# A decoder block with two token mixers: the loads of the keys for the gated states move from SP's queue to GpSimd's, and ahead of the first branch's weights

## The chip, the cores and the metric

The kernel runs on one core of a Trainium2 chip. Its time is the device time of one execution in microseconds (us). Before the change it is 1404.6 us, the median of 3 runs (1404.36 to 1404.93).

In what follows PE is TensorE, DVE is VectorE, ACT is ScalarE, POOL is GpSimd and SP is SyncE, which here does nothing but issue DMAs. An engine works off its instructions in the order in which they stand, and the DMAs that it issues stand in that order too: an instruction whose semaphore isn't there yet holds up all that stand behind it.

## The reference

One layer of a decoder block on 1024 rows of width 1024, in fp32. One input projection feeds two mixers, whose outputs are projected, gated and added.

```python
def mixing_sublayer(xn, w_in, b_gate, w_alpha_up, b_alpha, gla_norm_g, w_branch_sb, w_branch_gla, w_out):
    proj = xn @ w_in
    (sb_q, sb_k, sb_v, g_q, g_k, g_v, g_r, g_a, gate_sb, gate_gla) = jnp.split(proj, offsets, axis=-1)
    o_sb = stick_breaking_attention(...)     # 8 heads of 64, causal, weights are products of sigmoids
    o_gla = gla_chunked(...)                 # 4 heads, states of 64 x 128
    o_gla = o_gla * lax.rsqrt(jnp.mean(o_gla * o_gla, axis=-1, keepdims=True) + EPS)
    o_gla = from_heads(o_gla) * gla_norm_g * jax.nn.silu(g_r)
    y = (jax.nn.sigmoid(gate_sb + b_gate[0]) * (o_sb @ w_branch_sb)
         + jax.nn.sigmoid(gate_gla + b_gate[1]) * (o_gla @ w_branch_gla))
    return y @ w_out

def gla_chunked(q, k, v, log_a):             # per chunk of rows
    q_dec, k_inv, k_to_end = qf * jnp.exp(cum), kf * jnp.exp(-cum), kf * jnp.exp(cum_last - cum)
    o_intra = tril(q_dec @ k_inv.T) @ vf
    d_state = k_to_end.T @ vf                # added to the decayed state, chunk after chunk
    o_inter = q_dec @ states_before
```

The block then is h = x + mixing(rms_norm(x)), h = h + conv_ffn(rms_norm(h)) with 2 x 2816 channels, and a last RMSNorm.

## The kernel before

**Matmuls.** A fp32 product is made of three fp32r matmuls: each operand is split in a high part (a cast on ACT, L119) and the rest (a subtraction on DVE, L110). `mac` (L191, its matmul is L197) does the three products for every 128 rows of the contraction; a half output of 128 x 512 over 512 rows is 12 matmuls, and `branch` issues them as two groups of six.

**Stages.** (1) RMSNorm and the input projection; its outputs go to DRAM, among them `kt_d`, the keys of the gated branch that have been decayed to the end of their chunk (k_to_end). (2) The stick-breaking attention, in `attend`: `weigh`, `turn_weights` and `gather`. `gather` multiplies the weights with the values (L712), adds a bias on ACT (L718) and stores to `osb_d` with SP (L720). After the last head of a half of the rows, `fetch_heads` loads that half back with eight loads (L702), adds two partial sums each (DVE, L116) and splits them into `ob[0]` or `ob[1]`, the right operand of the first branch; `ob[1]` is made from the last two gathers' stores. In between, single steps of `gates` fill PE: the matmuls of the merge gates (L197), a sigmoid (ACT, L588) and a store to `gate_d` (L589). (3) The gated branch: `gated` interleaves `states` (per chunk of 128 rows a matmul on the keys, L808, a copy or an update of the state on DVE, L815 or L817, and a scaled copy on POOL, L819) with `out_pair` (L823 to L883). One `fill(first_branch, ...)` in two of three of its steps adds the first branch's matmuls, `o_sb @ w_branch_sb`. (4) `branch(1, ...)`, the output projection and the FFN.

**What sets the order around the change.** The code runs once to record the instructions; the order in which Python calls things is the order on each engine, except that the gates' matmuls are recorded at a lower priority (`tc.high_priority(offset=-LATER)`), so a scheduler may move them back behind others. Generators (`gate_steps`, `first_branch`) are drawn on with `fill(steps, n)`, which takes n steps. Between the end of `attend` and `gated` stand these lines:

```python
    first_branch = branch(0, ob, w_branch_sb)
    fill(first_branch, 1)
    fill(gate_steps, BEFORE)
    fetch_rest()
    fill(gate_steps, 128)
```

The first step of `first_branch` asks for the first branch weights (512 KB, `load`, L173, on SP) and makes two pieces of them (`piece`, L119 on ACT, L110 on DVE). `fetch_rest` asks for the keys: two loads of 512 KB from `kt_d` (L800), with `nc.sync.dma_start`, so in SP's queue. `gates` with 128 steps uses up what is left of the gates. `fetch_gated` (L783), called earlier from `gates`, has by then asked for the values, the decayed queries and the inverse keys on POOL's queue (L788, L790, L791).

**Buffers.** Keys, branch weights, gate weights and the attention's weights all take a buffer of the same tag, `t4` (128 x 1024 fp32); who asks first gets the one that came free first, and its load waits until the last reader of that buffer is done.

Of the kernel before, what the change touches and what calls it, by code (L numbers as in the profile page):

```python
# [17 lines left out]
P = 128  # L18
# [28 lines left out]
SPOT = 0  # L47
SOON = 1
FFN_FROM = 18
BEFORE = 4  # L50
PAIR_SKEW = 3
GLA = 2, 3
WAIT = 1, 1, 5, 4, 1
# [12 lines left out]
def block_kernel(ctx: ExitStack, tc: tile.TileContext, x, norm_mix_g, w_in, b_gate, w_alpha_up, b_alpha,  # L66
                 gla_norm_g, w_branch_sb, w_branch_gla, w_out, norm_ffn_g, w_ffn_in, conv_w, conv_b,
                 w_ffn_out, norm_final_g, out):
    nc = tc.nc
# [17 lines left out]
    def t8(dt=F32R):  # L87
        return sb.tile([P, 2 * D], dt, tag="t8", name=nm("t8"), bufs=16)

    def t4(dt=F32):  # L90
        return sb.tile([P, D], dt, tag="t4", name=nm("t4"), bufs=T4)

    def t2(dt=F32):
        return sb.tile([P, HALF], dt, tag="t2", name=nm("t2"), bufs=T2)

    def bank():
        return ps.tile([P, HALF], F32, tag="bank", name=nm("bank"), bufs=8)

    def dram(name, rows, cols, dt=F32):
        return dp.tile([rows, cols], dt, tag=name, name=name)  # L100

    def by(a, k):
        return a.rearrange("p (k c) -> p k c", k=k)

    def quarter():

        return [by(t8(), 4) for _ in range(2)]
# [4 lines left out]
    def mul(o, a, b):  # L112
        nc.vector.tensor_tensor(out=o, in0=a, in1=b, op=ALU.mult)

    def add(o, a, b):
        nc.vector.tensor_tensor(out=o, in0=a, in1=b, op=ALU.add)  # L116

    def split(h, l, src):
        nc.scalar.copy(h, src)  # L119
        sub(l, src, h.bitcast(F32))  # L120
# [38 lines left out]
    qd_d, ki_d, kt_d = (dram(n, GH * GK, S) for n in ("qd_d", "ki_d", "kt_d"))  # L159
# [6 lines left out]
    def fill(steps, n):  # L166
        for _ in range(n):
            next(steps, None)


    def load(src, k, room=None):
        raw = by((t4() if room is None else room)[:, 0:k * src.shape[1]], k)
        nc.sync.dma_start(raw, src.rearrange("(k p) c -> p k c", p=P))  # L173
        return raw
# [5 lines left out]
    def piece(src):  # L180

        v = t4(F32R)
        h, l = v[:, 0:HALF], v[:, HALF:]
        k = src.shape[1] if len(src.shape) == 3 else 1
        split(*((h, l) if k == 1 else (by(h, k), by(l, k))), src)
        return by(h, 4), by(l, 4)
# [4 lines left out]
    def mac(w, r, k=4, pt=None, start=True, stop=True):  # L191

        pt = bank() if pt is None else pt
        (wh, wl), (rh, rl) = w, r
        for kk in range(k):
            for m, (a, b) in enumerate(((wh, rh), (wh, rl), (wl, rh))):
                nc.tensor.matmul(pt, a[:, kk], b[:, kk], start=start and kk == 0 and m == 0,  # L197
                                 stop=stop and kk == k - 1 and m == 2)
        return pt
# [355 lines left out]
    def gates():  # L555

        def raw(n):
            if n < len(order):
                g = order[n][0]
                return load(w_in[:, C_GATE + g * P:C_GATE + (g + 1) * P], NK)  # L560

        gs = range(N_GATES, 2 * NK)
        order = [(g, (0,)) for g in gs[:N_HALVES]]
        order += [(g, (0, 1)) for g in gs[N_HALVES:]] + [(g, (1,)) for g in gs[:N_HALVES]]
        nxt = raw(0)
        ws = piece(nxt[:, :4]), piece(nxt[:, 4:])
        coming = None
        yield
        for n, (g, halves) in enumerate(order):
            if n == len(order) - N_HALVES:  # L570
                r = None
                for a in ("11", "12"):
                    del xq[a]
                fetch_gated()
            nxt = raw(n + 1)
            for half in halves:
                pt = bank()
                for kh in range(2):
                    for k in (0, 2):
                        w, r = ([a[:, k:k + 2] for a in v] for v in (ws[kh], xq[f"{half + 1}{kh + 1}"]))  # L580
                        with tc.high_priority(offset=-LATER):
                            mac(w, r, 2, pt, start=kh == 0 and k == 0, stop=kh == 1 and k == 2)
                        if half == halves[-1] and nxt is not None and 2 * kh + k // 2 == SOON:
                            coming = piece(nxt[:, :4]), piece(nxt[:, 4:])
                        if (kh, k) != (1, 2):
                            yield
                sg = t2()
                nc.scalar.activation(sg, pt, AF.Sigmoid, bias=col(V_BG, g))  # L588
                nc.scalar.dma_start(gate_d[g * P:(g + 1) * P, half * HALF:(half + 1) * HALF], sg)  # L589
                yield  # L590
            ws = coming

    gate_steps = gates()
# [200 lines left out]
    def fetch_rest():  # L794

        small = [by(t2(), 4) for _ in range(2)]
        state.extend((v[:, 0], v[:, 1]) for v in small)
        for p in range(2):
            kt = t4()
            nc.sync.dma_start(kt, kt_d[p * P:(p + 1) * P, :])  # L800
            gla[p] += by(kt, NT), by(t4(), NT)

    def states(p, n0, n1):
# [106 lines left out]
    def branch(b, o, w):  # L910

        def pieces(i):
            if i < NK:
                if i % 2 == 0:
                    raws.append(load(w[:, i * P:(i + 2) * P], 4))
                return piece(raws[-1][:, :, i % 2 * P:(i % 2 + 1) * P])

        raws = []
        nxt = [pieces(i) for i in range(2)]
        yield  # L920
        for n in range(2 * NK):
            i, th = n // 4 * 2 + n % 2, n // 2 % 2
            if n % 4 == 0:
                wps, nxt = nxt, []
            elif n % 4 > 1:
                nxt.append(pieces(i + 2))
            wp = wps[i % 2]
            sg = t2()
            g = b * NK + i
            nc.sync.dma_start(sg, gate_d[g * P:(g + 1) * P, th * HALF:(th + 1) * HALF])  # L930
            if i % 4 == 0:
                if b == 0:
                    yb[th, i // 4] = by(t8(F32), 4)
                else:
                    yq[th, i // 4] = quarter()
            pt = bank()
            mac([a[:, 0:2] for a in wp], [a[:, 0:2] for a in o[th]], 2, pt, stop=False)
            yield
            mac([a[:, 2:4] for a in wp], [a[:, 2:4] for a in o[th]], 2, pt, start=False)
            y = yb[th, i // 4][:, i % 4]  # L940
            if b == 0:
                mul(y, pt, sg)
            else:
                mul(sg, pt, sg)
                add(sg, sg, y)
                split(*(a[:, i % 4] for a in yq[th, i // 4]), sg)
            yield
# [34 lines left out]
    for w in attend():  # L982
        owed += w + EACH
        done += w
        rate = FILL[done > 3 * NT * (NT + 1) // 2 * SBH // 4]
        while owed >= rate:
            owed -= rate
            fill(gate_steps, 1)
    first_branch = branch(0, ob, w_branch_sb)
    fill(first_branch, 1)  # L990
    fill(gate_steps, BEFORE)
    fetch_rest()
    fill(gate_steps, 128)
    xq.clear()
    og = [quarter() for _ in range(2)]
# [320 lines left out]
```

## Time and profile before

| | |
|---|---|
| median of 3 runs | 1404.6 us (1404.36 to 1404.93) |
| profiled execution, its own time | 1404.87 us |
| its span in the profile | 1403.2 us |
| mean granted clock of TensorE | 0.996 |
| busy: PE, DVE, ACT, POOL | 1372.2, 1063.9, 643.6, 128.8 us |
| loads of the keys (L800) | 2 of 512 KB on SP's queue, 7.0 us from issue to landing |
| the first of them issued, landed | 547.88, 554.85 us from the span's start |

The profile is that of one execution. Each view gives places in us from the start of the span. A row of the timeline has start, length, engine, line, operation, output and input, the count, and in brackets how long the engine had been idle and what it waited for. A row of waits has the engine and the tile that waited, the operation waited for, then the sum, the count and the longest. In the chain that ended last each row is a piece of time and what it was spent in; "SPq L702" is SP issuing a DMA of line 702. A row of windows has the stretch, its length, the busy time of PE, PEld (weight loads), DVE, ACT and POOL, the granted clock of TensorE as a share of the full one, the busy share of the DMA engines, and GB/s. Matmuls are pipelined: a row's end overlaps with the next one's start.

### The profile page before, as it was taken

To read this page: it belongs to the slowest core of one execution; us is meant where nothing else is said; L and a number is where in the kernel's file an instruction comes from. 1 tells how busy PE (TensorE), PEld (TensorE's weight loads), DVE (VectorE), ACT (ScalarE), POOL (GpSimd) and SP (SyncE) were. 2 spreads that over 40 slices of the span, in tenths; PEclk is the share of its full clock that TensorE was granted. 3 is DMA by queue.
4 is the path that set the end of the run, shared out by engine and by line. 5 is a ranking of instruction groups with operands and counts; after the bars stand their busy time and mean duration, and the time that the engine had idled before them with its cause. 6 is when DMAs were issued, how large, how long until landed. Compare 5 with 4: busy or idle time off the path is not lost.

```text
span 1403.2 us, 18305 instructions
## 1 busy us (share of the span) xinstructions
PE 1372.2 (98%) x6549; PEld 1138.5 (81%) x6549; DVE 1063.9 (76%) x1640; ACT 643.6 (46%) x1242; POOL 128.8 (9%) x223
## 2 busy tenths in 40 slices
PE   7999999999999996999999999999999999999998
PEld 5788888888888875888888788888888888888886
DVE  6388788874878775648447997998888987897855
ACT  6234455653766563543234543333333333454654
POOL 0002133103011000300000000100000000000000
PEclk9999999999999998999999999999999999999999
DMA  6335277448766475464424434563554437953232
GB/s 241 139 97 167 70 231 247 143 157 231 194 150 152 127 223 196 148 213 158 155 91 135 114 96 150 190 217 134 180 181 150 152 108 267 324 176 99 97 106 105
DMA packets 165082, 228.44 MB, mean 163 GB/s; under 512 B 11017, under 2 KB 106379, under 8 KB 164480
## 3 DMA queue, kind: packets, MB, share of 16 engines
q1 hardware_dynamic: 136496, 141.63, 33.0%
q0 software_dynamic: 21920, 71.63, 15.6%
q10 hardware_dynamic: 6576, 14.03, 2.7%
q8 instruction: 51, 0.84, 0.3%
q14 instruction: 39, 0.32, 0.1%
HBM read 160.80 MB, written 66.45 MB: 162 GB/s over the span
## 4 chain that ended last, share of the span: by engine, by line
PE 56%; DVE 3%; DMA 1%; ACT 1%; issue 1%; SPq 0%; POOL 0%; ACTq 0%; DVEq 0%
PE bank L197 34%; PE bank L1179 15%; PE bank L1046 5%; DVE t L110 2%; DVE t L116 1%; DMA t<-kt_d 0%; PE bank L808 0%; DMA t<-gate_d 0%; PE bank L845 0%; DMA t<-in_w_branch_sb_dram 0%; DMA t<-in_w_branch_gla_dram 0%; PE bank L321 0%; PE bank L880 0%; SPq L702 0%; DVE t L313 0%
## 5 line engine op out<-in xcount | busy, mean ns | idle before, releaser
L197 PE MATMUL bank<-t,t 128*128 128x512 f32 x3624 | 862.9, 393 | 0.9 <-DVE t L110 0.8
L197 PEld LDWEIGHTS bank<-t,t 128*128 128x128 f32 x3624 | 677.1, 188 | 143.3 <-DVE t L110 1.6
L110 DVE TENSOR_TENSOR t<-t,t 128x512 fp32r<-128x512 f32 (+3 forms) x663 | 440.3, 697 | 93.9 <-ACT t L119 88.7
L119 ACT CAST t<-t 128x512 fp32r<-128x512 f32 x551 | 325.1, 626 | 342.1 <-DVE t L110 84.0
L116 DVE TENSOR_TENSOR t<-bank,t 128x512 f32<-128x512 f32 x266 | 179.3, 685 | 101.6 <-PE bank L197 58.3
L1179 PE MATMUL bank<-t,t 128*128 128x512 f32 x924 | 209.6, 389 | 0.0
L1179 PEld LDWEIGHTS bank<-t,t 128*128 128x128 f32 x924 | 173.4, 188 | 36.0
L110 DVE TENSOR_TENSOR t<-bank,t 128x512 fp32r<-128x512 f32 (+4 forms) x128 | 72.1, 578 | 33.2 <-ACT t L119 32.8
L367 PE MATMUL bank<-t,t 128*128 128x512 f32 x384 | 91.7, 398 | 1.6 <-ACT t L119 1.5
L1046 PE MATMUL bank<-t,t 128*128 128x512 f32 x384 | 88.9, 391 | 0.0
L116 DVE TENSOR_TENSOR t<-t,t 128x512 f32<-128x512 f32 x115 | 75.5, 685 | 15.8 <-ACT t L497 8.6
L367 PEld LDWEIGHTS bank<-t,t 128*128 128x128 f32 x384 | 72.9, 191 | 17.9 <-ACT t L119 2.2
L1077 ACT ACTIVATE t<-t,vcol 128x1024 f32<-128x1024 f32 x22 | 27.4, 1245 | 128.0 <-DVE t L116 128.0
L110 DVE TENSOR_TENSOR t<-t 128x512 f32<-128x512 f32 x120 | 82.1, 691 | 3.7 <-DMA t<-in_w_ffn_in_dram 3.3
L119 ACT CAST t<-bank 128x512 fp32r<-128x512 f32 (+3 forms) x124 | 61.8, 511 | 49.1 <-PE bank L691 27.3
L1046 PEld LDWEIGHTS bank<-t,t 128*128 128x128 f32 x384 | 71.6, 188 | 14.7
L1079 DVE SCALAR_TENSOR_TENSOR t<-t,vcol,t 128x1023 f32<-128x1023 f32 (+1 forms) x44 | 56.2, 1278 | 14.1 <-ACT t L1077 13.9
L682 DVE TENSOR_TENSOR_SCAN t<-t,t 128x128 f32<-128x128 f32 (+1 forms) x64 | 51.4, 814 | 14.4 <-ACT t L679 13.7
L691 PE MATMUL bank<-ident,t 128*128 128x128 f32 x288 | 53.5, 273 | 1.9 <-ACT t L588 1.3
L677 PE MATMUL bank<-t,t 128*128 128x128 f32 (+3 forms) x192 | 54.6, 368 | 0.1
L712 PE MATMUL bank<-t,t 128*128 128x256 f32 (+1 forms) x320 | 51.1, 276 | 0.4 <-DVE t L110 0.4
L712 PEld LDWEIGHTS bank<-t,t 128*128 128x128 f32 x320 | 46.4, 190 | 2.8 <-DVE t L110 0.6
(142 smaller groups left out, 760.4 us busy)
## 6 DMA issues: line engine op xcount, KB each, us to landing
t<-in_w_ffn_in_dram SPq DMA_DIRECT2D x50, 512.0 KB, 4.5
t<-in_w_in_dram SPq DMA_DIRECT2D x43, 512.0 KB, 5.8
act_d<-t POOLq DMA_DIRECT2D x22, 512.0 KB, 5.9
t<-in_w_ffn_out_dram SPq DMA_DIRECT2D x22, 512.0 KB, 7.1
wsum_d<-t POOLq DMA_DIRECT2D x22, 512.0 KB, 3.8
t<-act_d SPq DMA_DIRECT2D x22, 512.0 KB, 5.6
t<-wsum_d SPq DMA_DIRECT2D x44, 256.0 KB, 3.2
t<-in_w_ffn_out_dram SPq DMA_DIRECT2D x33, 256.0 KB, 2.6
```

What stands on the lines that cost most here:

```text
L110: nc.vector.tensor_tensor(out=o, in0=a, in1=b, op=ALU.subtract)
L116: nc.vector.tensor_tensor(out=o, in0=a, in1=b, op=ALU.add)
L119: nc.scalar.copy(h, src)
L197: nc.tensor.matmul(pt, a[:, kk], b[:, kk], start=start and kk == 0 and m == 0, stop=stop and kk == k - 1 and m == 2)
L367: nc.tensor.matmul(pt, a[:, k % 4, t], b, start=k == 0 and m == 0, stop=k == NK - 1 and m == 2)
L677: nc.tensor.matmul(z[:, 0:w], q[:, a, e, ts_], kk[:, e, b0 * P:b1 * P], start=a == 0, stop=a == 1)
L682: nc.vector.tensor_tensor_scan(out=kr, data0=kr, data1=above[:, 0:w], initial=1.0, op0=ALU.mult, op1=ALU.max)
L691: nc.tensor.transpose(pt[:, b * P:(b + 1) * P], ke[:, b * P:(b + 1) * P], ident)
L712: nc.tensor.matmul(po[:, c0:2 * P], vt[b][:, head, :], a[b // 4][:, b % 4, c0:], start=(b == 0 and n == 0), stop=(b == nb - 1 and n == 1))
L1046: nc.tensor.matmul(pt, a[:, k % 4, t], b, start=(k == 0 and m == 0), stop=(k == NK - 1 and m == 2))
L1079: nc.vector.scalar_tensor_tensor(out=cv[:, i:], in0=av[:, :S - i], scalar=col(V_CW, (2 - i) * NF + f), in1=cv[:, i:], op0=ALU.mult, op1=AL ...
L1179: nc.tensor.matmul(pts[m][i], a[:, t], b, start=(k == 0 and x_ == 0), stop=(k == NH - 1 and x_ == 2))
```

## The change

The loads of the keys are issued by POOL instead of SP. `fetch_rest` is called directly after `attend`, ahead of `branch(0, ...)`, so ahead of the request for the first branch's weights. The constant `BEFORE` and the four gate steps that it placed ahead of `fetch_rest` go; all steps are still taken, by `fill(gate_steps, 128)`. Line numbers of the changed kernel are lower by one from L51 to the third edit.

```diff
@@ -47,7 +47,6 @@
 FFN_FROM = 18
-BEFORE = 4
 PAIR_SKEW = 3
@@ -797,7 +796,7 @@
         for p in range(2):
             kt = t4()
-            nc.sync.dma_start(kt, kt_d[p * P:(p + 1) * P, :])
+            nc.gpsimd.dma_start(kt, kt_d[p * P:(p + 1) * P, :])
             gla[p] += by(kt, NT), by(t4(), NT)
@@ -986,10 +985,9 @@
             fill(gate_steps, 1)
+    fetch_rest()
     first_branch = branch(0, ob, w_branch_sb)
     fill(first_branch, 1)
-    fill(gate_steps, BEFORE)
-    fetch_rest()
     fill(gate_steps, 128)
```

On PE, at the end of the attention, before the change: `bank_5267` is the last gather, `bank_5246` the last output of the gates, `bank_5360` the first state, and `bank_5368` the first branch's first output (a count at a row's end is of equal rows in sequence).

```order
L712 MATMUL bank_5267<-t_993_5087,t_580_3278 128x128
L197 MATMUL bank_5246<-t_538_3111,t_1004_5146 128x512
L197 MATMUL bank_5246<-t_55_322,t_1005_5149 128x512
L197 MATMUL bank_5246<-t_56_323,t_1005_5149 128x512
L197 MATMUL bank_5246<-t_55_322,t_1005_5149 128x512 x2
L197 MATMUL bank_5246<-t_56_323,t_1005_5149 128x512
L197 MATMUL bank_5246<-t_55_322,t_1005_5149 128x512 x2
L197 MATMUL bank_5246<-t_56_323,t_1005_5149 128x512
L197 MATMUL bank_5246<-t_55_322,t_1005_5149 128x512 x2
L197 MATMUL bank_5246<-t_56_323,t_1005_5149 128x512
L197 MATMUL bank_5246<-t_55_322,t_1005_5149 128x512
L808 MATMUL bank_5360<-t_960_4954,t_1040_5350 128x256
```

And the same place after it:

```order
L711 MATMUL bank_5267<-t_993_5087,t_580_3278 128x128
L807 MATMUL bank_5360<-t_960_4954,t_1036_5327 128x256
L196 MATMUL bank_5246<-t_538_3111,t_1004_5146 128x512
L196 MATMUL bank_5246<-t_55_322,t_1005_5149 128x512
L196 MATMUL bank_5246<-t_56_323,t_1005_5149 128x512
L196 MATMUL bank_5246<-t_55_322,t_1005_5149 128x512
L196 MATMUL bank_5368<-t_967_4986,t_1041_5335 128x512
L196 MATMUL bank_5368<-t_968_4987,t_1041_5335 128x512
L807 MATMUL bank_5375<-t_960_4954,t_1038_5330 128x256
L196 MATMUL bank_5368<-t_967_4986,t_1041_5335 128x512 x2
L196 MATMUL bank_5368<-t_968_4987,t_1041_5335 128x512
L196 MATMUL bank_5368<-t_967_4986,t_1041_5335 128x512
```

The first matmul on the keys has moved ahead of the last 13 gate matmuls, and these are now in two parts, four ahead of the first branch's first matmuls, and nine below these rows, behind the twelve of its first output. The second keys' matmul (`bank_5375`) stands two matmuls into that output.

On POOL, where `fetch_gated`'s loads end, before and after (`emid` is the scale of L819, which is L818 after the change):

```order
L788 DMA t_962_4959<-gv_d 128x4x512
L790 DMA t_961_4958<-qd_d 128x1024
L791 DMA t_961_4958<-ki_d 128x1024
L819 TENSOR_SCALAR t_1041_5352<-t_1038_5348,emid_976 128x128
L819 TENSOR_SCALAR t_1043_5355<-t_1039_5349,emid_977 128x128
```

```order
L789 DMA t_961_4958<-qd_d 128x1024
L790 DMA t_961_4958<-ki_d 128x1024
L799 DMA t_1036_5327<-kt_d 128x1024
L799 DMA t_1038_5330<-kt_d 128x1024
L818 TENSOR_SCALAR t_1037_5329<-t_1034_5325,emid_976 128x128
L818 TENSOR_SCALAR t_1039_5332<-t_1035_5326,emid_977 128x128
```

The two loads of keys stand behind the loads of `fetch_gated`, with nothing in between, and ahead of POOL's first work on the states.

On ACT, at the last gather, before: the casts from `bank_5253` and `bank_5260` are of the attention's weights, those from `t_1034_5325` of the first branch's weights, the L718 row is the last gather's bias, and the L588 row a gate's sigmoid.

```order
L119 CAST t_991_5085<-bank_5253 128x4x128
L119 CAST t_990_5084<-bank_5260 128x4x128
L119 CAST t_1035_5327<-t_1034_5325 128x512
L718 ACTIVATE t_1023_5284<-bank_5267,t_473_2874 128x128 x2
L119 CAST t_1036_5330<-t_1034_5325 128x512
L119 CAST t_1024_5289<-t_1026_5291 128x512
L588 ACTIVATE t_1037_5345<-bank_5246,vcol 128x512
```

And after it, where the branch weights are `t_1040_5333`:

```order
L118 CAST t_991_5085<-bank_5253 128x4x128
L118 CAST t_990_5084<-bank_5260 128x4x128
L717 ACTIVATE t_1023_5284<-bank_5267,t_473_2874 128x128 x2
L118 CAST t_1041_5335<-t_1040_5333 128x512
L118 CAST t_1042_5338<-t_1040_5333 128x512
L118 CAST t_1024_5289<-t_1026_5291 128x512
```

The last gather's two activations were behind the first cast of the branch weights and are now ahead of it.

## The prediction

> **What bounds the kernel now.** I read the share of each engine first, then what PE waited for, then PE's timeline at the longest wait, and from there followed the chain of waits backwards. Of PE:
>
> ```profile
> PE 1372.2 (98%) x6549; PEld 1138.5 (81%) x6549; DVE 1063.9 (76%) x1640; ACT 643.6 (46%) x1242; POOL 128.8 (9%) x223
> PE bank L808 <- DMA t<-kt_d: 11.1, 1, 11.1
> PE bank L321 <- DVE t L313: 7.9, 1, 7.9
> ```
>
> PE is busy 98% of the span, so what isn't a wait of PE is hardly worth anything, and its longest wait, 11.1 us, is for the loads that the change moves. PE's timeline there (start, length, idle before):
>
> ```profile
> 538.93 1.89 PE L712 MATMUL bank<-t,t 128*128 128x256 f32 x15
> 540.66 3.21 PE L197 MATMUL bank<-t,t 128*128 128x512 f32 x13
> 554.98 1.19 PE L808 MATMUL bank<-t,t 128*128 128x256 f32 x2 [11.11 <-DMA t<-kt_d]
> ...
> 564.99 1.27 PE L197 MATMUL bank<-t,t 128*128 128x512 f32 x4
> ```
>
> The last gathers are followed by 13 gate matmuls, and at 543.87 PE stops until the keys have landed. The row at 564.99 is the first matmul on `ob[1]`; from it on the order is the same before and after, so I measure the change by how much earlier that matmul starts. What SP did meanwhile:
>
> ```profile
> 543.24 1.09 SPq L720 DMA_DIRECT2D osb_d<-t  x2
> 544.42 3.41 SPq L702 DMA_DIRECT2D t<-osb_d  x7
> 547.88 1.03 SPq L800 DMA_DIRECT2D t<-kt_d  x2
> ...
> 551.64 0.38 SPq L173 DMA_DIRECT2D t<-in_w_branch_sb_dram  x1
> ```
>
> The keys stood in SP's queue behind the last stores and seven loads of `osb_d`. Nothing but this order made them late. The restart costs something more, as the chain that ended last shows, beside the granted clock (column before the last two):
>
> ```profile
> 547.88 6.97 DMA t<-kt_d
> 554.98 1.19 PE bank L808 x2
> 556.17 2.41 PE bank L197 x6
> ...
> 559.44 1.39 PE bank L197 x6
> 560.83 0.43 PE bank L808 x2
> ```
> ```profile
> 532.00:538.00 6.00, 6.00 (x41) 5.27 (x40) 3.44 (x6) 3.28 (x8) 0.00 (x0) 1.00 0.21 67
> 544.00:550.00 6.00, 0.00 (x0) 0.00 (x0) 1.75 (x4) 1.21 (x2) 0.00 (x0) 0.84 0.71 229
> 550.00:555.00 5.00, 0.02 (x1) 0.05 (x1) 3.27 (x6) 1.82 (x3) 0.00 (x0) 0.50 0.93 346
> 555.00:558.00 3.00, 3.00 (x7) 2.44 (x8) 1.27 (x3) 0.04 (x1) 0.37 (x1) 0.50 1.06 392
> ```
>
> In the idle time the clock fell to 0.50 and stayed there to 558. The same work took 1.19 instead of 0.43 (one L808) and 2.41 instead of 1.39 (six L197), 1.78 us lost.
>
> **The change part by part.** *The ceiling.* If nothing waited, PE would from 540.66 do seven L808 (7 x 0.43 = 3.01), the 13 gate matmuls (13 x 1.39/6 = 3.01) and four groups of six first-branch matmuls (4 x 1.39 = 5.56): 11.58, and start on `ob[1]` at 552.24 instead of 564.99. That is 12.75 us: the wait of 11.11 and 1.64 of clock, close to the 1.78 above. No more than this can be won here.
>
> *When the keys land.* Their buffers come free with DVE's last split of a gate weight, and the loads then need POOL:
>
> ```profile
> 531.07 1.28 DVE L110 TENSOR_TENSOR t<-t,t 128x512 fp32r<-128x512 f32 x2
> 494.79 0.53 POOL L791 DMA_DIRECT2D t<-ki_d  x1
> 557.09 0.37 POOL L819 TENSOR_SCALAR t<-t,emid 128x128 f32<-128x128 f32 x1 [61.78 <-DMA t<-kt_d]
> ```
> ```profile
> DMA to landing us min/median/max: 4.2/6.7/9.2
> DMA to landing us min/median/max: 4.9/7.7/10.5
> ```
>
> The split ends at 532.35. POOL has done nothing since 495.32 and its next work, L819, needs the keys itself, so nothing is queued behind the two issues (0.53 each, as L791's). They start at about 532.4 and 532.9. The two rows on landing are those of L790 and L791, loads of the same 512 KB through the same queue: 4.2 to 10.5 us. So the first keys land between 536.6 and 542.9 (by the medians 539 to 540), the second by 543.4; PE asks for them at about 540.9 and 543.3. I take no wait, by the medians and because the DMA share was 0.21 at 532 to 538, and keep 2.0 as the other end. Then PE would come to `ob[1]` at 554.3 at the latest, which is no more than 0.3 behind what the next but one paragraph finds there anyway.
>
> *The first weights (W1).* The ACT rows:
>
> ```profile
> 542.07 0.62 ACT L119 CAST t<-t 128x512 fp32r<-128x512 f32 x1 [4.56 <-DMA t<-in_w_branch_sb_dram]
> 542.59 0.62 ACT L718 ACTIVATE t<-bank,t 128x128 f32<-128x128 f32 x2
> ...
> 559.61 1.14 ACT L119 CAST t<-t 128x512 fp32r<-128x512 f32 x2 [4.57 <-DMA t<-in_w_branch_sb_dram]
> ```
>
> The load of those weights is not moved; its cast ends at 542.69. After one L808 and four gate matmuls (0.43 + 0.93) PE is there at 542.02: it waits 0.67 and would come to `ob[1]` at 552.91.
>
> *The last heads (W2).* In before ACT stood waiting for the weights with the last two L718 behind the cast. In after they are ahead of it and can start when the gathers end, at 540.85: 1.74 sooner, and with them the stores, the seven loads behind them and the pieces of `ob[1]` made of these. DVE's rows of before:
>
> ```profile
> 549.39 0.69 DVE L110 TENSOR_TENSOR t<-t,t 128x512 fp32r<-128x512 f32 x1 [0.68 <-ACT t L119]
> 551.72 0.69 DVE L116 TENSOR_TENSOR t<-t,t 128x512 f32<-128x512 f32 x1 [1.03 <-DMA t<-osb_d]
> 555.07 0.69 DVE L110 TENSOR_TENSOR t<-t,t 128x512 fp32r<-128x512 f32 x1 [0.69 <-ACT t L119]
> 556.21 0.61 DVE L815 COPY t<-bank 64x128 f32<-64x128 f32 x2 [0.45 <-PE bank L808]
> ```
>
> The last piece was ready at 555.76, so now at 554.02. What is new is that four copies of L815 (two pairs, 1.22) stand between these pieces on DVE. They fit into its waits (0.68 + 1.03 + 0.69 = 2.40): I take nothing, and at most the whole 1.22. The other way, the loads of `osb_d` no longer share the DMA engines with 1 MB of keys (0.71 to 0.93 of their time): PE could be as early as 552.91. So PE goes on between 552.9 and 555.2, likeliest at 554.0, 11.0 us earlier than before. Its waits are short now (1.1 at most), so I leave the clock full.
>
> *What is late next.* The second load of branch weights left SP at 551.64 and its cast began 8.0 us later. PE wants it two outputs on, 24 matmuls (5.56) after 554.0: not before 559.6. SP no longer issues the keys ahead of it (1.03), so it leaves by 550.6 and, after the same 8.0, its first piece is cast at 559.2; with the stores 1.74 earlier, at 557.5. That covers it by 0.4 to 2.1 us. If it left no earlier than before, it would cost 560.23 - 559.6 = 0.6.
>
> Sum: the profiled execution took 1404.87 (span 1403.2 and 1.67 around it), 0.27 above the median of the three runs. 1404.87 - 11.0 = 1393.9; own range 1392.1 (ceiling) to 1395.1.
>
> **The rivals.** *B, only part of it.* The last pieces of `ob[1]` or the next weights come late: DVE's copies cost their whole 1.22 and the stores leave no sooner, so the last piece is ready at 555.76 + 1.22 = 556.98; 8.0 us are left, 1396.9. For it: PE then stands in the same stretch of SP's queue as before. Against: ACT's order.
>
> *C, given back later.* PE could meet an engine that is late regardless. DVE is that one:
>
> ```profile
> 620.00:700.00 80.00, 80.00 (x356) 66.27 (x355) 48.31 (x75) 20.05 (x34) 0.00 (x0) 1.00 0.52 179
> 770.00:780.00 10.00, 9.99 (x49) 7.96 (x48) 10.00 (x18) 7.08 (x14) 0.00 (x0) 1.00 0.91 233
> ```
>
> DVE (third busy figure) is full at 770 to 780, and if its work there didn't come forward, all 11 us would go: 1404.9. Against: from 620 to 700 it has 31.7 of 80 us free, and what it works on at 770 is what PE gives it.
>
> *D, slower.* The keys on POOL's queue come later than on SP's. The 13 gate matmuls, which covered 3.2 us before, now stand behind the first L808, so a late load holds them too. With the wait long enough to lose the clock again, PE comes to `ob[1]` 11.58 + 1.64 after the keys: level at 564.99 - 13.22 = 551.77, 19.4 us after asking, 1.8 times the longest landing of a POOL load (10.5). From 554.6 the time is more than 0.2% (2.8 us, about what a measurement of this kernel can tell from none) above before. What could do it is DVE holding up the writing of POOL's descriptors: DVE's rows around 531 touch each other, and it is busy 3.44 of the 6 us after. At 25 us, 2.4 times the longest row, the keys land at 557.4, PE comes to 570.6 and the time is 1410.5. Against:
>
> ```profile
> 480.00:495.00 15.00, 15.00 (x99) 13.43 (x98) 9.39 (x16) 8.60 (x24) 2.56 (x5) 1.00 0.67 190
> ```
>
> the POOL loads of the last two landings were asked for beside a DVE that was busy 9.39 of 15, and took no more than 10.5. The Trainium skill, "SBUF — State Buffer", in the section on a bandwidth-pool intuition, says that a DMA whose descriptors GpSimd writes took 3100 ns instead of 620 beside a DVE copy, five times as long, because the two engines lock each other out of a shared port. By that rule, as an estimate, the shortest landing, 4.2, would become 21 us: keys at 553.4, `ob[1]` at 566.6, 1406.5. The rows above speak against it here.
>
> *E, it doesn't do what it says.* If the keys' buffers came free late, or POOL's loads landed with the last ones of SP, nothing would be gained: 1404.9. The row at 531.07 speaks against.
>
> **How the numbers follow.** A as summed 0.72 (1393.9), B 0.14 (1396.9), C 0.06 and E 0.03 (both 1404.9), D 0.05 (1410.5). A and B are faster: 0.86; C and E the same: 0.09; D slower: 0.05. The range goes from 1391.8, the ceiling counted from the median (1404.6 - 12.75), to 1398.0, B with another 1.1 of wait; it leaves out C, D and E and little else.
>
> **What would show it.** In the profile after: keys asked for at about 532 on POOL and landed by 543; PE's wait for them at L808 gone or under 2 us; a wait of about 0.7 for the first branch weights and one of about 1 for the last piece of `ob[1]`; the clock at 1.00 through 540 to 560; the first matmul on `ob[1]` near 554.0, and the same 11 us in all places behind it. It would be wrong if PE still idled more than 5 us between 540 and 565, if the landing took over 15 us, or if a later place came less early than this one.

## The result, and the profile after

| | before | changed |
|---|---|---|
| median of 5 runs | 1404.93 us (1404.36 to 1407.20) | 1396.19 us (1394.55 to 1399.61) |
| profiled execution, its own time | 1404.87 us | 1396.35 us |
| its span | 1403.2 us | 1394.5 us |
| mean granted clock | 0.996 | 0.998 |

The ratio is 0.9935 with an interval from 0.9923 to 0.9946: 9.1 us faster, between 7.6 and 10.8. The forecast was 1393.9, in a range from 1391.8 to 1398.0. The changed kernel's lines are one lower: L807 is the matmul on the keys (L808 before), L814 the copy of a first state, L196 the matmul of `mac`. In the experiments, lines that an edit adds shift the numbers behind them again.

What PE waited for after the change:

```profile
PE bank L196 <- ACT t L118: 1.4, 1, 1.4
...
PE bank L844 <- POOL t L836: 0.7, 1, 0.7
...
PE bank L196 <- DVE t L814: 0.2, 1, 0.2
```

The 11.1 us for the keys are gone, and three small waits are new: 1.4, 0.7 and 0.2. PE's timeline from the last gathers on:

```profile
540.36 1.89 PE L711 MATMUL bank<-t,t 128*128 128x256 f32 x15
542.09 0.65 PE L807 MATMUL bank<-t,t 128*128 128x256 f32 x2
542.38 1.27 PE L196 MATMUL bank<-t,t 128*128 128x512 f32 x4
545.05 0.73 PE L196 MATMUL bank<-t,t 128*128 128x512 f32 x2 [1.40 <-ACT t L118]
...
555.73 1.63 PE L196 MATMUL bank<-t,t 128*128 128x512 f32 x6 [0.21 <-DVE t L814]
...
596.98 1.16 PE L844 MATMUL bank<-t,t 128*128 128x128 f32 x8 [0.65 <-POOL t L836]
```

The last gathers start at 540.36, where they started at 538.93 before: this execution was 1.43 us behind already ahead of the change. So that such shifts don't enter, everything below is measured by the distance from the start of that row (x15) to the first matmul on `ob[1]`: before 564.99 - 538.93 = 26.06, after 555.73 - 540.36 = 15.37, that is 10.7 us less. From there to the end 0.4 to 0.6 is given back: the row at 596.98 stood at 605.84 before, which is 8.86 earlier, or 10.3 with the 1.43; of the whole span it is 8.7 + 1.43 = 10.1. This is how before looked at that place:

```profile
605.84 1.16 PE L845 MATMUL bank<-t,t 128*128 128x128 f32 x8
```

The keys on POOL, and from their issue to landing:

```profile
537.00 1.12 POOL L799 DMA_DIRECT2D t<-kt_d  x2 [40.05 <-PE bank L690]
```
```profile
DMA to landing us min/median/max: 4.0/4.5/5.0
```

The first lands at 541.0, ahead of its matmul at 542.09, and the second at 542.6, ahead of the second matmul on keys, which stands two of the first branch's matmuls behind 545.05. The request for the first branch weights on SP, ACT at the last gather, and the windows (the clock stands ahead of the last two figures, the DMA engines' share and GB/s):

```profile
539.60 0.46 SPq L172 DMA_DIRECT2D t<-in_w_branch_sb_dram  x1
```
```profile
542.29 0.63 ACT L717 ACTIVATE t<-bank,t 128x128 f32<-128x128 f32 x2 [3.36 <-PE bank L711]
544.38 1.14 ACT L118 CAST t<-t 128x512 fp32r<-128x512 f32 x2 [1.47 <-DMA t<-in_w_branch_sb_dram]
```
```profile
538.00:544.00 6.00, 5.65 (x33) 4.52 (x31) 1.87 (x3) 1.55 (x4) 0.12 (x1) 1.00 0.97 332
544.00:550.00 6.00, 4.95 (x22) 4.13 (x23) 2.57 (x4) 1.76 (x3) 0.00 (x0) 1.00 0.85 264
```

And before, SP and the first of the two windows:

```profile
538.02 0.54 SPq L173 DMA_DIRECT2D t<-in_w_branch_sb_dram  x1
```
```profile
538.00:544.00 6.00, 5.88 (x33) 4.79 (x31) 1.38 (x3) 1.66 (x4) 0.00 (x0) 1.00 0.49 152
```

The last gather's activations follow the gathers at once (542.29) and the clock stays at 1.00. The keys' transfer has moved into 538 to 544, where the DMA engines' share is 0.97 and was 0.49. The cast of the first branch weights starts 4.78 us after their issue (544.38 - 539.60), where it was 4.05 (542.07 - 538.02).

### The profile page after: what moved, and what is told of

It is laid out like the page before. It is cut to its first block, busy times and chain, and to the rows that moved or that the text cites. A ratio compares the mean times of both kernels' runs of the same rounds, so it can differ in the third digit from the quotient of the medians.

```text
span 1394.5 us, 18313 instructions
## 1 busy us (share of the span) xinstructions
PE 1371.5 (98%) x6549; PEld 1138.3 (82%) x6549; DVE 1063.7 (76%) x1640; ACT 643.8 (46%) x1242; POOL 127.7 (9%) x225
## 4 chain that ended last, share of the span: by engine, by line
PE 57%; DVE 3%; DMA 1%; ACT 1%; issue 0%; SPq 0%; POOL 0%; ACTq 0%; DVEq 0%
PE bank L196 35%; PE bank L1177 15%; PE bank L1044 5%; DVE t L109 2%; DVE t L115 1%; PE bank L844 0%; DMA t<-osb_d 0%; DMA t<-in_w_branch_sb_dram 0%; DMA t<-gate_d 0%; PE bank L879 0%; PE bank L320 0%; PE bank L807 0%; PE bank L831 0%; ACT t L118 0%; PE bank L856 0%
## 5 line engine op out<-in xcount | busy, mean ns | idle before, releaser
L196 PE MATMUL bank<-t,t 128*128 128x512 f32 x3624 | 862.0, 393 | 2.5 <-ACT t L118 1.4
L196 PEld LDWEIGHTS bank<-t,t 128*128 128x128 f32 x3624 | 676.2, 188 | 145.2 <-ACT t L118 2.3
```

## The experiments

Each line of the table is one kernel. Each ratio is to runs of before in the same round, whose median was 1404.9 to 1405.9 us. "Start" is the last gathers' row, "distance" is from there to `ob[1]`, and "span" is the span's difference to 1403.2 less that of the start to 538.93.

| kernel | median us, runs | ratio to before (interval) | start | distance | span |
|---|---|---|---|---|---|
| before, again | 1405.5, 1 | | 539.85 | 25.91 | -0.3 |
| changed | 1396.19, 5 | 0.9935 (0.9923 to 0.9946) | 540.36 | 15.37 | -10.1 |
| changed, again | 1396.64, 5 | 0.9935 (0.9922 to 0.9947) | 539.26 | 15.44 | -10.1 |
| the queue alone | 1400.84, 6 | 0.9969 (0.9958 to 0.9980) | 540.33 | 20.21 | -4.4 |
| the place alone | 1396.85, 5 | 0.9941 (0.9927 to 0.9954) | 540.17 | 16.69 | -8.8 |
| the queue, and ACT's order | 1395.66, 5 | 0.9925 (0.9911 to 0.9938) | 540.23 | 14.66 | -10.1 |
| ACT's order alone | 1403.86, 11 | 0.9988 (0.9979 to 0.9997) | 543.78 | 24.48 | -1.8 |
| changed, gates first | 1394.85, 5 | 0.9923 (0.9911 to 0.9936) | 539.51 | 15.60 | -10.3 |
| changed, copies on ACT | 1395.55, 5 | 0.9935 (0.9921 to 0.9948) | 544.88 | 14.87 | -11.2 |
| changed, both, gates broken up | 1394.48, 5 | 0.9922 (0.9909 to 0.9934) | 540.09 | 16.90 | -9.2 |
| changed, both, gates in one piece | 1395.11, 5 | 0.9928 (0.9914 to 0.9942) | 540.46 | 13.31 | -11.5 |

The queue alone and ACT's order alone can be told from the rest by their times. The other seven kernels can't be told from each other: their intervals are some 3.5 us wide. The distances can, though each stands for one trace: the two traces of before differ by 0.15, the two of the changed kernel by 0.07.

**The queue alone.** Before, with one word changed:

```diff
-            nc.sync.dma_start(kt, kt_d[p * P:(p + 1) * P, :])
+            nc.gpsimd.dma_start(kt, kt_d[p * P:(p + 1) * P, :])
```

> The kernel before, with the keys' two loads on GpSimd's queue and nothing else changed (their place in the code and BEFORE stay). Measure: from the start of the last gathers' row to the first matmul on ob[1]; before 564.99 - 538.93 = 26.06 us, after the whole change 555.73 - 540.36 = 15.37. Theory (the stall was SP's order alone): the keys are asked for at about 534 and there before PE's last gate matmul ends, the 11.1 us wait goes, and with before's order on ACT the pieces of ob[1] come 1.7 us later than in the changed kernel: 16 to 17 us, 9 to 10 us faster than before. Rival (the earlier place is what brings the keys): the keys' buffers come free late or the loads land beside the last loads of osb_d, a wait of over 3 us for them stays, and the distance is over 19 us.

```profile
540.33 1.89 PE L712 MATMUL bank<-t,t 128*128 128x256 f32 x15
...
553.93 0.70 PE L808 MATMUL bank<-t,t 128*128 128x256 f32 x2 [1.18 <-ACT t L588]
...
557.24 0.67 PE L808 MATMUL bank<-t,t 128*128 128x256 f32 x2 [1.22 <-DVE t L815]
560.54 2.29 PE L197 MATMUL bank<-t,t 128*128 128x512 f32 x6 [2.63 <-DVE t L815]
```
```profile
545.65 0.62 ACT L119 CAST t<-t 128x512 fp32r<-128x512 f32 x1 [6.75 <-DMA t<-in_w_branch_sb_dram]
546.17 0.62 ACT L718 ACTIVATE t<-bank,t 128x128 f32<-128x128 f32 x2
```

Neither theory had this. No wait for keys is left, as the first said, but the distance is that of the second. Half the gain has turned into other waits. The first branch weights now share the DMA engines with the keys, they land 6.2 us after their issue, and in before's order on ACT the last gather's activations stand behind their cast: these began 546.17 - 542.22 = 3.95 us after the gathers' end, and the stores, the loads of `osb_d` and DVE's pieces with them. The states' copies stand behind those pieces on DVE, and PE waits for the copies.

The last of these waits, 2.63 us, also cost the clock:

```profile
562.00:564.00 2.00, 2.00 (x8) 1.15 (x9) 1.84 (x7) 0.63 (x2) 0.75 (x2) 0.50 1.10 386
```

The six matmuls behind it took 2.29 us, where before's at the same place took 1.73. So of the 5.9 us won up to `ob[1]` (26.06 - 20.21) the span has only 4.4.

**The place alone.** The changed kernel with the keys on SP again:

```diff
-            nc.gpsimd.dma_start(kt, kt_d[p * P:(p + 1) * P, :])
+            nc.sync.dma_start(kt, kt_d[p * P:(p + 1) * P, :])
```

> The changed kernel, with the keys' loads put back on SP's queue, so that only their place is new. Theory (any place ahead of the last loads of osb_d is enough): SP issues them at about 538 in before's places, ahead of the first branch weights, which leave 1.0 us later; the keys land at 542.5 to 545, PE waits 1 to 3 us for them and under 1 us for the weights, and the distance from the last gathers to ob[1] is 15.5 to 17.5 us: 8.5 to 10.5 us faster than before, up to 2 slower than the change. Rival (it takes GpSimd's queue): the stores ahead of them on SP hold the keys up, the distance stays over 20 us.

```profile
540.17 1.89 PE L711 MATMUL bank<-t,t 128*128 128x256 f32 x15
...
543.34 0.67 PE L807 MATMUL bank<-t,t 128*128 128x256 f32 x2 [0.99 <-DMA t<-kt_d]
...
556.86 1.63 PE L196 MATMUL bank<-t,t 128*128 128x512 f32 x6 [1.74 <-DVE t L814]
```

As the first theory had it: 16.69, with 0.99 of wait for the keys, at the low end of what it named. Without GpSimd's queue, 9.4 of the 10.7 us are there. By the counts in the trace the gates' matmuls stand ahead of the first branch here; the next run shows that this by itself changes little.

**The gates first.** On the changed kernel, `LATER` is taken off the last gate steps, so that all 13 matmuls stand ahead of the first branch:

```diff
-                        with tc.high_priority(offset=-LATER):
+                        with tc.high_priority(offset=-later[0]):
...
+    later[0] = 0
     fetch_rest()
```

> The changed kernel, with the gates' last matmuls recorded without their lower priority, so that all 13 stand between the first matmul on the keys and the first branch's first matmuls (in the change four do). They cover the wait of 1.4 us for the first branch weights that the changed kernel's trace shows. Theory as predicted (the last piece of ob[1] sets the place at which PE goes on): what PE gains it waits for again there; the distance stays at 15.2 to 15.5 us and the time is that of the change within 0.3. Rival (the wait for the weights is on the path, and ob[1] was hardly late): 14.0 to 14.5 us, 1.0 to 1.4 faster than the change.

```profile
539.51 1.89 PE L712 MATMUL bank<-t,t 128*128 128x256 f32 x15
...
541.54 5.02 PE L196 MATMUL bank<-t,t 128*128 128x512 f32 x19
...
555.11 1.63 PE L196 MATMUL bank<-t,t 128*128 128x512 f32 x6 [1.80 <-DVE t L815]
```
```profile
554.67 0.29 DVE L815 COPY t<-bank 64x128 f32<-64x128 f32 x1
...
555.99 0.68 DVE L109 TENSOR_TENSOR t<-t,t 128x512 fp32r<-128x512 f32 x1
```

The wait for the weights is gone (19 matmuls without a break) and turned up again at `ob[1]`: 1.80 there instead of 0.21. The 1.4 us were not on the path: the distance, 15.60, is 0.1 above the range expected and that of the change within 0.25. PE started 0.15 us behind the end of the copy (554.67 + 0.29 = 554.96), while DVE made the last piece of `ob[1]` only at 555.99.

**The copies on ACT.** On the changed kernel:

```diff
-                    nc.vector.tensor_copy(new[r], src)
+                    with tc.high_priority(offset=200):
+                        nc.scalar.copy(new[r], src)
```

> The changed kernel, with the four copies of the first states (L814) on ScalarE at a raised priority instead of on VectorE. In the changed kernel's trace the first matmul on ob[1] waits 0.21 us for the last of these copies, whose bank it takes, and not for a piece of ob[1]. Theory (it waits for the bank): the wait goes, the distance is 14.7 to 15.1 us, 0.2 to 0.6 less than the change. Rival, as predicted (the last piece of ob[1] sets the place): VectorE's pieces end at most 1.2 us earlier without the copies among them, and a wait for a piece shows at L196; or, if ScalarE is now late with its casts, it is over 15.4 us.

```profile
544.88 1.89 PE L711 MATMUL bank<-t,t 128*128 128x256 f32 x15
...
559.75 1.73 PE L196 MATMUL bank<-t,t 128*128 128x512 f32 x6
```

No wait at `ob[1]`, and 14.87. So PE had waited for the copy, DVE's last work there, and not for the pieces. Of what the two instructions touch, only a bank can tie them, which the copy reads and the next output takes; no run shows the bank itself.

**Both, twice.** The two edits together:

> The gates first and the copies on ScalarE together (both edits of the two runs ahead, on the changed kernel). Alone the first left the distance from the last gathers to ob[1] where it was (15.60 us, PE waiting 1.80 for the last copy instead of 1.4 for the weights), the second took 0.50 off it (14.87). Theory (two waits one behind the other, of which each hides the other's removal): both gone, PE runs through in 13.3 to 14.0 us, 1.4 to 2.0 faster than the change at this place. Rival (the pieces of ob[1] come next): 14.6 to 15.0 us, no better than the copies alone.

```profile
540.09 1.89 PE L712 MATMUL bank<-t,t 128*128 128x256 f32 x15
...
545.74 4.85 PE L196 MATMUL bank<-t,t 128*128 128x512 f32 x13 [1.90 <-ACT t L118]
...
556.99 1.73 PE L196 MATMUL bank<-t,t 128*128 128x512 f32 x6
```
```profile
546.00:548.00 2.00, 2.00 (x6) 1.56 (x6) 1.42 (x3) 0.21 (x1) 0.00 (x0) 0.54 0.89 305
548.00:550.00 2.00, 2.00 (x7) 1.53 (x7) 1.32 (x3) 1.34 (x3) 0.00 (x0) 0.61 1.00 345
```

Neither theory: the copies' priority had shifted the order, one first-branch matmul stood among the gate matmuls, by the trace behind the sixth, PE waited 1.90 us for the weights there, and the clock fell to 0.54 and 0.61. One more edit puts the gates in one piece:

```diff
-    later[0] = 0
+    later[0] = -4
```

> The two edits together once more, now with the gates' last 13 matmuls really in one piece: in the run before one of the first branch's matmuls stood behind the seventh of them, PE waited 1.90 us there for the weights, the clock fell to 0.54 to 0.61 from 546 to 550, and the distance became 16.90 us. Theory (two waits, each hiding the other's removal): no wait for the weights, none for the copies' bank, the clock stays, 13.3 to 14.0 us, 1.4 to 2.0 less than the change. Rival (the pieces of ob[1], or the casts on ScalarE behind the copies, come next): 14.5 us or more, no better than the copies alone (14.87).

```profile
540.46 1.89 PE L712 MATMUL bank<-t,t 128*128 128x256 f32 x15
...
542.48 4.88 PE L196 MATMUL bank<-t,t 128*128 128x512 f32 x19
...
553.77 1.73 PE L196 MATMUL bank<-t,t 128*128 128x512 f32 x6
...
557.27 1.13 PE L833 MATMUL bank<-t 64*128 64x128 f32 x14 [0.84 <-DVE t L818]
```

13.31 us, which is the prediction's ceiling to the hundredth (552.24 - 538.93): no wait is shown up to `ob[1]`. Of the 2.06 us by which it beats the change there, 1.4 are left in the span, after a new wait of 0.84. The two waits did hide each other. By its traced place it is the best version; its time, 1395.11 with the ratio at 0.9928, doesn't show it.

**ACT's order.** A dependency that only sets the order puts the first cast of the branch weights behind the last gather's second activation, first on the kernel with the queue alone:

```diff
+        seen['cast'] = nc.scalar.copy(h, src)
...
+            seen['bias'] = nc.scalar.activation(o[:, c], po[:, c], AF.Identity, bias=vend[:, i:i + 1])
...
+                if b == i == 0:
+                    after(seen['cast'], seen['bias'])
```

> The kernel with the keys on GpSimd's queue alone, and on ScalarE the last gather's two activations ahead of the first cast of the branch weights, as they are in the changed kernel; nothing else moves on ScalarE there. With the queue alone the distance was 20.21 us, and those activations began 3.95 us after the gathers' end, behind a cast whose weights landed only 6.2 us after their issue. Theory (this order is what the queue alone lacks): they begin at the gathers' end, the stores and all behind them come 3 to 4 us sooner, and the distance is 16 to 17 us, 3 to 4 us faster than with the queue alone. Rival (the keys' traffic itself makes the loads of osb_d late): over 18.5 us.

```profile
540.23 1.89 PE L713 MATMUL bank<-t,t 128*128 128x256 f32 x15
...
554.89 1.62 PE L198 MATMUL bank<-t,t 128*128 128x512 f32 x6
```
```profile
542.16 0.63 ACT L719 ACTIVATE t<-bank,t 128x128 f32<-128x128 f32 x2 [3.37 <-PE bank L713]
```
```profile
554.45 0.29 DVE L816 COPY t<-bank 64x128 f32<-64x128 f32 x1
```

14.66: all that the queue alone had lost, 5.55 us, more than expected, and 0.7 less than the change itself. Here too PE starts 0.15 us behind the end of the last copy; that copy ends 14.5 us behind the start of the last gathers (554.74 - 540.23), and in the change 15.2 (555.58 - 540.36), which is the 0.7. Some of it is lost again later; the spans are the same. Then as the only edit on before:

> The kernel before with that order on ScalarE as the only edit: the keys stay on SP's queue behind the last loads of osb_d. Theory (stores 1.74 us sooner, and with them the seven loads and the keys behind them): the wait for the keys falls from 11.1 to 9.2 to 9.6 us, the distance from 26.06 to 24.2 to 24.6, the time by 1.5 to 1.9. Rival (the keys' landing is bound by the DMA engines and not by their issue): the keys land where they did, within 0.5 us.

```profile
543.78 1.89 PE L713 MATMUL bank<-t,t 128*128 128x256 f32 x15
...
558.25 1.19 PE L809 MATMUL bank<-t,t 128*128 128x256 f32 x2 [9.52 <-DMA t<-kt_d]
...
568.26 1.73 PE L198 MATMUL bank<-t,t 128*128 128x512 f32 x6
```

24.48: 1.6 us, and the wait for the keys 9.52, as expected. The same order is worth 1.6 us with the keys on SP and 5.5 with the keys on POOL.

**The same kernels again.**

> The changed kernel once more. Its profiled execution was 1.42 us behind that of before already ahead of the change, of which 1.06 at the very start and 0.72 at 362 us arose in places that both kernels share. Theory (this is the execution and not the change): here the time ahead of the change differs from it by some tenths to some us either way, while the distance from the last gathers to ob[1] stays at 15.2 to 15.6 us. Rival (the changed program makes it): 1.2 to 1.6 us again, in the same places.

```profile
539.26 1.89 PE L711 MATMUL bank<-t,t 128*128 128x256 f32 x15
...
554.70 1.63 PE L196 MATMUL bank<-t,t 128*128 128x512 f32 x6 [0.23 <-DVE t L814]
```

> The kernel before once more, for a second trace of it. Theory (the times ahead of the change differ from one execution to the next): its last gathers start some tenths to some us after 538.93, with the same 26.0 to 26.2 us from there to ob[1] and the same wait of 11.0 to 11.2 for the keys. Rival (before is always early there): 538.8 to 539.1.

```profile
539.85 1.89 PE L712 MATMUL bank<-t,t 128*128 128x256 f32 x15
...
555.89 1.19 PE L808 MATMUL bank<-t,t 128*128 128x256 f32 x2 [11.10 <-DMA t<-kt_d]
...
565.76 1.73 PE L197 MATMUL bank<-t,t 128*128 128x512 f32 x6
```

The time ahead of the change belongs to the execution: 0.33 behind 538.93 now and not 1.43, and before's second one 0.92. The profile that the forecast was added to is the earliest of the twelve. The two latest, 543.78 and 544.88, had lost time at one place: PE waited there 2.02 and 2.53 us for ACT at 361 to 365, and the clock fell behind it. They are also the slowest runs of their kernels (1407.98 and 1399.72 us).

## Why the prediction was right

*What bounds the kernel.* Right: with the keys asked for earlier, by either part, the wait of 11.1 us goes (0.99 is left with the place alone), and in the change the clock stays at 1.00. With the queue alone it fell all the same, behind a wait that the prediction didn't have. The gain at `ob[1]`, 10.7 us, was forecast at 11.0.

*When the keys land.* Forecast at 536.6 to 542.9 and by 543.4; with the 1.43 of this execution taken off, 539.6 and 541.2. It came about differently: they were asked for at 537.0, 3.2 later than DVE's split (533.79 here) would allow, and took 4.0 and 5.0 and not the medians 6.7 and 7.7. Rival D, slower by late keys, didn't come. The rule weighed there (the Trainium skill, "SBUF — State Buffer", the section on a bandwidth-pool intuition: five times as long beside a DVE copy) was hardly put to the test: when the change's loads were issued DVE was idle. In the kernel with the queue alone they were issued beside DVE's subtractions and landed after 4.5 and 5.4 us; no copy ran there.

*The first weights (W1).* Mis-sized: 0.67 forecast, 1.40 measured. I left the time from issue to cast unchanged at 4.05 us, though the keys' 1 MB moved right beside it; it became 4.78, which is the difference. As the gates-first run shows, it cost nothing in the end.

*The last heads (W2).* The number was right and the reason wrong, so that it fitted is luck. "PE goes on when the last piece of `ob[1]` is ready" gave 554.02, here 555.45, and PE went on at 555.73. But the last piece wasn't what it waited for:

```profile
554.58 0.67 DVE L109 TENSOR_TENSOR t<-t,t 128x512 fp32r<-128x512 f32 x1
555.29 0.29 DVE L814 COPY t<-bank 64x128 f32<-64x128 f32 x1
```

It was the copy behind that piece. I had taken the four copies at nothing since they fit into DVE's waits; I didn't ask who waits for them. Nor does the first group of six matmuls need the last piece: with the gates first it was made 0.9 us behind PE's start (555.99 and 555.11).

*ACT's order.* Taken at 1.74, and alone it is 1.6. That it would be worth 5.5 on the new queue, and so is what makes the change a whole one and not half, the prediction didn't see: it took the order for a part of the sum and not for the cover of a new delay.

*Given back later* (rival C): 0.4 to 0.6 of the 10.7, not at 770 but at 597, where PE waits 0.65 for POOL. "A later place came less early" was one of the prediction's signs of being wrong, and this much of it came true.

*The sum.* 1404.87 - 11.0 = 1393.9; from the same execution, 1404.87 - 10.1 = 1394.8. The other 1.4 up to 1396.19 I put down to the spread of the executions; the interval of the gain, 7.6 to 10.8, holds the 10.1. The start of the last gathers alone came 0.3 to 6.0 us later than in before's first profile, in kernels that are the same up to there.

## What to carry to other kernels

Before a load is moved away from a queue, list what it will now travel beside, and on which engine something unrelated stands behind the transfer that becomes slower; here an order on ACT made the difference between 5.9 and 11.4 us. When PE waits for "the last piece", check also whose bank its next output takes. And measure an edit of under 1% by a distance within the trace as well: it was good to 0.15 us where five runs were good to some 1.7.

## What the runs showed of the hardware that was not expected

A short wait can cost the clock. After 1.90 us of idle PE it was 0.54 to 0.61 for 4 us, and 13 matmuls took 4.85 us where they took 3.21 in before (both edits, gates broken up). The waits of 2.63 us (the queue alone), 2.53 (copies on ACT, at 362) and 2.02 (ACT's order alone, at 361) were each followed by a clock of 0.50 as well. Behind waits of 1.74 and 1.80 us six matmuls took 1.63, as behind the change's wait of 0.21, and the clock stayed at 1.00. So in these twelve traces, from 18 us to 1385, each idle time of PE of 1.90 us or more was followed by a fall, and none of 1.80 or less was. Whether the bound lies there in general, and whether the work ahead matters, wasn't tried.

POOL started the keys' loads 3.2 us after DVE's split of a gate weight, which the prediction took for the last reader of their buffers: the split ends at 532.50 + 1.29 = 533.79, and the loads start at 537.00.

```profile
532.50 1.29 DVE L109 TENSOR_TENSOR t<-t,t 128x512 fp32r<-128x512 f32 x2
```

The same 3.2 us stand in the four kernels made from the changed one by the gates and the copies. But in the two kernels with the keys on POOL at their old place it is 4.4 (533.77 to 538.19, and 533.65 to 538.09), so it is no fixed delay behind that split. In the trace each of these loads also carries a wait for PE, and the profile names PE's transposes as what ended it. The transposes don't touch buffers of the tag `t4`; the attention's weights do lie in such buffers, and PE's gathers read them. Which of PE's instructions the loads waited for, and why, is open.
